# Where the operands of a matmul begin in SBUF: stationary tiles at multiples of 256 bytes, four ring slots at four different offsets

## The chip, the cores and the metric

The kernel runs on one core of one Trainium2 chip. The time is the device time of one launch in microseconds (us); of several runs the median is given. Beside it stands the span of one profiled execution, from the first to the last instruction of the program on that core.

## The reference

One layer of a decoder trunk on a sequence of 256 tokens of width 2048, all in float32:

```python
h = h + 0.5 * rms_norm(swiglu(rms_norm(h, w1), w_gate, w_up, w_down), w2)   # ffn1, D_FF = 5504
h = h + rms_norm(hybrid_token_mixer(rms_norm(h, w3), ...), w4)              # w_in is 2048 x 11280
h = h + 0.5 * rms_norm(swiglu(rms_norm(h, w5), w_gate, w_up, w_down), w6)   # ffn2
```

`swiglu(x)` is `(silu(x @ w_gate) * (x @ w_up)) @ w_down`. The mixer projects with `w_in`, runs two causal gated linear attentions (one with 4 heads, one with 8), normalises and gates their outputs, projects each with a 1024 x 2048 matrix (`w_branch_gla`, `w_branch_hgrn`), mixes the two with sigmoid gates and projects with `w_out` (2048 x 2048). Nearly all arithmetic is in the products of 256 tokens with these weight matrices.

## The kernel before

**Tiles.** The 256 tokens are two halves of 128 (`t` = 0, 1). A product `x @ w` is made in blocks of 512 output columns (`CB`): for each half, the block is one PSUM tile of 128 x 512, summed over the rows of `w` in steps of 128 (`kt`). TensorE holds a 128 x 128 piece of the transposed activations as its stationary operand and streams 512 columns of weights past it as the moving operand.

**Three matmuls per step.** Every float32 operand is split into a high part in the fp32r format and the rest, also fp32r (`split_into`, L118: ScalarE makes the high part at L119, VectorE the rest at L120). A product is then three matmuls (`mm3`, L122): high activations with high weights (L124), low activations with high weights (L125), high activations with low weights (L126). Each matmul is preceded on TensorE by the load of its stationary operand, which the profile shows as LDWEIGHTS on PEld. The three matmuls of one step have the stationary pieces `xhi`, `xlo`, `xhi` of the same `kt`, so the load that runs beside a matmul is always one for the next matmul's piece.

**The ring.** Weights come in chunks of 256 rows by 512 columns (`wchunk`, L105): one DMA of 512 KB into `raw`, then the split into `whi` and `wlo`. These three tags live in the pool `ring` with `bufs=4` (L80): each tag has four slots, side by side in each partition, and the chunks use them in turn. A chunk feeds 12 matmuls: 2 rows of 128, 2 halves of tokens, 3 matmuls each (`gemm_block`, L128, from L149; in `out_proj`, L248, a chunk is 128 rows by 1024 columns, again 12 matmuls). Some chunks of a product that has to wait for the second half's activations are kept longer, in tiles named `held`, outside the ring.

**The stationary operands.** `xhi` and `xlo` (`new_xT`, L192) hold the transposed input of a stage: 16 pieces of 128 columns, 512 bytes each in a partition. In the down projections of the FFNs the stationary operands are `hkhi` and `hklo` (L392 in `ffn`), in the two branch projections of the mixer they are the tiles `oT` (in `attention`, from the pool `b2`).

**Where these lie.** A pool places its tiles in the order in which they are allocated, and a tag's slot is as large as the tag's largest tile. The largest `whi` is that of the mixer's product of 16 + 512 columns: 2 x 528 x 4 = 4224 bytes = 16 x 256 + 128. A partition of SBUF is laid out so (bytes; the last column is the rest after division by 256):

| tiles | first bytes | mod 256 |
|---|---|---|
| `xhi`, `xlo` | 34048, 42240, 50432, 58624 | 0 |
| `whi`, four slots | 83712, 87936, 92160, 96384 | 0, 128, 0, 128 |
| `wlo`, four slots | 100608, 104832, 109056, 113280 | 0, 128, 0, 128 |
| `hkhi`, `hklo` | 167040, ... 181376 | 128 |
| `oT` and the mixer's `held` | 164000, ... | 160 |
| the FFNs' `held` | 183424, ... | 128 |

All pieces of a stationary tile and both halves of a ring tile are a multiple of 256 bytes apart, but for the one product of 528 columns (parts of 264 columns, 1056 bytes). The **offset** of a matmul is in what follows the first byte of its moving operand less that of the stationary operand which is loaded beside it, mod 256. With `xhi` at 0 the four slots have the offsets 0, 128, 0, 128; with `hkhi` at 128 they have 128, 0, 128, 0; with `oT` at 160 they have 96, 224, 96, 224.

**What sets the order.** The order of instructions on each engine is that in which the code issues them, with waits on tiles added by the framework; small jobs (norms, transposes, the attention) are generators that `Side` runs a step at a time between the chunks.

Of the kernel before, what the change touches and what calls it, by code (L numbers as in the profile page):

```python
# [7 lines left out]
F32 = mybir.dt.float32  # L8
F32R = mybir.dt.float32r
# [6 lines left out]
P = 128  # L16
D = 2048
NT = 2
KT = D // P
# [3 lines left out]
CB = 512  # L23
GATE_NORMALIZER = 16.0
LEVELS = (1, 2, 4, 8, 16, 32, 64)
TAIL = 4
STEPS = ((5, 3, 3, 3), (7, 3, 2, 2))
O_GQ, O_GK, O_GV, O_GO, O_CODE = 0, 512, 1024, 2048, 3072
O_HQ, O_HF, O_HI, O_HO, O_ZG, O_ZH = 3088, 4112, 5136, 6160, 7184, 9232
# [41 lines left out]
def kernel(ctx: ExitStack, tc: tile.TileContext, a: dict, out: bass.AP):  # L71
    nc = tc.nc
    side = Side()

    const = ctx.enter_context(tc.tile_pool(name="const", bufs=1))
    hpool = ctx.enter_context(tc.tile_pool(name="hpool", bufs=1))
    tpool = ctx.enter_context(tc.tile_pool(name="tpool", bufs=1))
    ring = ctx.enter_context(tc.tile_pool(name="ring", bufs=4))
    rows = ctx.enter_context(tc.tile_pool(name="rows", bufs=8))
    small = ctx.enter_context(tc.tile_pool(name="small", bufs=4))  # L80
    work = ctx.enter_context(tc.tile_pool(name="work", bufs=2))
# [4 lines left out]
    def nm(s):  # L86
        uid[0] += 1
        return f"{s}_{uid[0]}"

    def ps_tile(s="ps"):  # L90
        return psum.tile([P, CB], F32, tag="ps", name=nm(s))

    h = [[hpool.tile([P, CB], F32, name=f"h{t}_{n}") for n in range(4)] for t in range(NT)]
    ident = const.tile([P, P], F32, name="ident")
    nc.scalar.dma_start(ident, a["c_ident"])
    nhalf = const.tile([P, 4], F32, name="nhalf")
    nc.vector.memset(nhalf, -0.5)


    def ring_alloc(w):  # L100
        hi = ring.tile([P, 2, w], F32R, tag="whi", name=nm("whi"))
        lo = ring.tile([P, 2, w], F32R, tag="wlo", name=nm("wlo"))
        return [(hi, lo)]

    def wchunk(src: bass.AP, w: int, alloc=ring_alloc):  # L105

        raw = ring.tile([P, 2, w], F32, tag="raw", name=nm("raw"))
        nc.sync.dma_start(raw, src)
        parts = alloc(w)
        if len(parts) == 1:  # L110
            split_into(*parts[0], raw)
            hi, lo = parts[0]
            return [(hi[:, i, :], lo[:, i, :]) for i in range(2)]
        for i, (hi, lo) in enumerate(parts):
            split_into(hi, lo, raw[:, i, :])
        return parts
# [11 lines left out]
    def gemm_block(w_dram, c0, w, lhs, nkt=KT, held=None):  # L128
# [19 lines left out]
        if held is None:  # L148
            for k0 in range(0, nkt, 2):  # L149
                parts = chunk(k0, ring_alloc)  # L150
                for t in range(NT):
                    mm(t, k0, parts)
                side.pump()
        else:
            kept = []
            for i, k0 in enumerate(range(0, nkt, 2)):
                kept.append((k0, chunk(k0, ring_alloc if i < 4 else held)))
                mm(0, *kept[-1])
                side.pump()
            for k in kept:  # L160
                mm(1, *k)
                side.pump()
            side.flush()
# [89 lines left out]
    def out_proj(w_dram, nkt, lhs, post, scale, pre, held, after):  # L253
# [15 lines left out]
        def load(kt, hf, alloc=ring_alloc):  # L269
            return wchunk(w_dram[kt * P:(kt + 1) * P, hf * 1024:(hf + 1) * 1024]  # L270
                          .rearrange("p (n c) -> p n c", n=2), CB, alloc)

        def mm(t, n, kt, parts):
            if acc[t][n] is None:
                acc[t][n] = ps_tile(f"acc{t}{n}")
            mm3(acc[t][n], lhs(t, kt), parts[n % 2], kt == 0, kt == nkt - 1)

        order = [(kt, hf) for hf in range(2) for kt in range(2)]
        order += [(kt, hf) for kt in range(2, nkt - TAIL) for hf in range(2)]
        for i, (kt, hf) in enumerate(order):  # L280
# [6 lines left out]
            if i > 3 and early:  # L287
                o, x0, x1 = early.pop(0)
                nc.vector.tensor_tensor(o, x0, x1, op=ALU.mult)
        tail = [[(kt, load(kt, hf, held if hf else ring_alloc)) for kt in range(nkt - TAIL, nkt)]  # L290
                for hf in range(2)]
# [6 lines left out]
        def finish(t, ss):  # L298
# [23 lines left out]
            def ahead(n):  # L322
                tmp = scaled_acc(t, n, r1, wpre[n])
                nc.vector.tensor_tensor(u[t][n], u[t][n], tmp, op=ALU.add)
                if t == 0:
                    settle(n)
                    square(h[t][n], ss2, n)

            ahead(0)
            ahead(1)  # L330
            for n, steps in enumerate(STEPS[t]):
                for _ in range(steps):
# [10 lines left out]
        for t in range(NT):  # L343
            ss = small.tile([P, 4], F32, tag="ss", name=nm("ss"))
            for n in range(4):
                for i, (kt, parts) in enumerate(tail[n // 2]):
                    mm(t, n, kt, parts)
                    if i == TAIL // 2 - 1:
                        side.pump()
# [58 lines left out]
    def mixer(x, rs):  # L408
        xl = lhs_of(x)
        w_in = a["w_in"]  # L410
        with ExitStack() as mctx:
            mp = mctx.enter_context(tc.tile_pool(name="mp", bufs=1, reuse_waits="tile"))
            b2 = mctx.enter_context(tc.tile_pool(name="b2", bufs=1, reuse_waits="tile"))
            oT, state = {}, {}

# [343 lines left out]
            return out_proj(a["w_out"], KT, lhs_of(mT), "mix_post_norm", 1.0, "ffn2_pre_norm", held, after)  # L759


    warm = const.tile([P, 1], F32, name="warm")
    nc.scalar.activation(warm, nhalf[:, 0:1], AF.Silu)
    wrow = const.tile([KT, P], F32, name="wrow")
    nc.scalar.dma_start(wrow, a["ffn1_pre_norm"][0].rearrange("(k p) -> k p", p=P))
    wcol = const.tile([P, KT], F32, name="wcol")
    tp = ps_tile()
    nc.tensor.transpose(tp[:, :KT], wrow, ident[:KT, :KT])
    nc.vector.tensor_copy(wcol, tp[:, :KT])
# [1 line left out]
    for t in range(NT):  # L771
        side.spawn(first_norm(t, x, rs, wcol))
    x, rs = ffn("ffn1", x, rs, "ffn1_post_norm", "mix_pre_norm")
    x, rs = mixer(x, rs)
    ffn("ffn2", x, rs, "ffn2_post_norm", None)
    side.flush()
# [46 lines left out]
```

## Time and profile before

| | |
|---|---|
| median of 3 runs | 2230.61 us (2230.21 to 2231.8) |
| the profiled execution's own time | 2231.95 us |
| its span | 2230.2 us |
| mean granted TensorE clock | 0.999 |
| VectorE, ScalarE, GpSimd busy | 53%, 45%, 3% of the span |
| DMA | 410.24 MB, mean 184 GB/s |

The profile groups instructions by line, engine and tiles (`mm<-whi,xhi` is a matmul into the PSUM tile `mm` with `whi` moving and `xhi` stationary). In the timeline each row begins with the start in us and the duration in us. The ends of matmuls are modelled and overlap the next one's start, so the cost of a matmul is read from start to start: the time from one row's start to that of the 12th row after it, divided by 12, is the pitch of a chunk's matmuls.

### The profile page before, as it was taken

Reading aid. Unit: us, or ns where it says so; the run is one execution under the profiler, and the core shown is the slowest. Engines: PE = TensorE matmul, PEld = TensorE weight load, DVE = VectorE, ACT = ScalarE, POOL = GpSimd, SP = SyncE. Lnnn points to the kernel's source line nnn. Section 1 sums busy time; section 2 is a strip of 40 time slices with the busy share of each in tenths; the row PEclk is TensorE's granted clock in tenths of the full one; section 3 lists DMA queues with packets and bytes.
Section 4 is the critical chain, followed back from the end, with each engine's and each line's share of the span. In section 5 each row is a group of like instructions: output and inputs, shape, how many; then the busy total and the mean of one; then the engine's idle time right before and its main releaser. Section 6 shows DMA issues by size and latency. Waiting matters only on the chain.

```text
span 2230.2 us, 26313 instructions
## 1 busy us (share of the span) xinstructions
PE 2203.3 (99%) x10197; PEld 1815.4 (81%) x10197; DVE 1184.1 (53%) x1278; ACT 994.3 (45%) x1202; POOL 69.2 (3%) x106
## 2 busy tenths in 40 slices
PE   8999999999999999999999999999999999999998
PEld 6888888897888788888888888878888888898886
DVE  5544444446445744657575656465444444444455
ACT  5444444444444564444434444354444444444443
POOL 0000000000000400000000000021000000000001
PEclk9999999999999999999999999999999999999999
DMA  6655555566555556554545765555555565566663
GB/s 228 189 184 186 188 188 185 187 204 205 191 189 197 160 172 189 170 150 143 155 153 175 232 204 184 184 166 182 189 186 187 184 189 189 170 217 190 191 192 135
DMA packets 189344, 410.24 MB, mean 184 GB/s; under 512 B 13681, under 2 KB 22289, under 8 KB 189218
## 3 DMA queue, kind: packets, MB, share of 16 engines
q1 hardware_dynamic: 183712, 400.21, 57.0%
q10 hardware_dynamic: 5506, 8.34, 1.2%
q8 instruction: 80, 1.31, 0.2%
q14 instruction: 46, 0.38, 0.0%
HBM read 406.41 MB, written 2.10 MB: 183 GB/s over the span
## 4 chain that ended last, share of the span: by engine, by line
PE 64%; DVE 1%; DMA 1%; POOL 1%; ACT 0%; issue 0%; ACTq 0%; POOLq 0%; DVEq 0%
PE mm L124 16%; PE mm L126 16%; PE mm L125 16%; PE acc L126 5%; PE acc L124 5%; PE acc L125 5%; PE ps L187 1%; PE ps L531 1%; DMA raw<-in_w_out_dram 0%; PE ps L581 0%; PE ps L538 0%; PE ps L515 0%; DVE tmp L295 0%; DVE wlo L120 0%; DMA raw<-in_w_in_dram 0%; POOL h L303 0%
## 5 line engine op out<-in xcount | busy, mean ns | idle before, releaser
L120 DVE TENSOR_TENSOR wlo<-raw,whi 128x1024 fp32r<-128x1024 f32 (+2 forms) x740 | 899.5, 1217 | 916.0 <-ACT whi L119 880.2
L119 ACT ACTIVATE whi<-raw 128x1024 fp32r<-128x1024 f32 (+2 forms) x740 | 777.3, 1051 | 1134.2 <-PE mm L125 814.9
L124 PE MATMUL mm<-whi,xhi 128*128 128x512 f32 (+2 forms) x2096 | 817.1, 390 | 3.5 <-ACT whi L119 3.3
L126 PE MATMUL mm<-wlo,xhi 128*128 128x512 f32 (+2 forms) x2096 | 810.1, 387 | 5.5 <-DVE wlo L120 5.5
L125 PE MATMUL mm<-whi,xlo 128*128 128x512 f32 (+2 forms) x2096 | 809.0, 386 | 0.2
L126 PEld LDWEIGHTS mm<-wlo,xhi 128*128 128x128 f32 x2096 | 393.7, 188 | 87.3 <-DVE wlo L120 7.2
L124 PEld LDWEIGHTS mm<-whi,xhi 128*128 128x128 f32 x2096 | 394.1, 188 | 83.1 <-ACT whi L119 3.7
L125 PEld LDWEIGHTS mm<-whi,xlo 128*128 128x128 f32 x2096 | 394.4, 188 | 79.9 <-DVE xlo L120 1.6
L124 PE MATMUL acc<-whi,hkhi 128*128 128x512 f32 x656 | 257.5, 392 | 0.8 <-ACT hT L376 0.8
L126 PE MATMUL acc<-wlo,hkhi 128*128 128x512 f32 x656 | 257.5, 393 | 0.0
L125 PE MATMUL acc<-whi,hklo 128*128 128x512 f32 x656 | 257.3, 392 | 0.0
L124 PEld LDWEIGHTS acc<-whi,hkhi 128*128 128x128 f32 x656 | 123.2, 188 | 28.8 <-ACT hT L376 1.2
L126 PEld LDWEIGHTS acc<-wlo,hkhi 128*128 128x128 f32 x656 | 123.1, 188 | 28.1 <-DVE wlo L120 0.2
L125 PEld LDWEIGHTS acc<-whi,hklo 128*128 128x128 f32 x656 | 123.1, 188 | 27.9
L217 POOL TENSOR_TENSOR v<-ss 128x1 f32<-128x1 f32 x12 | 6.2, 518 | 1693.2 <-ACT sq L228 1692.4
L124 PE MATMUL mm<-whi,oT 128*128 128x512 f32 x128 | 51.3, 401 | 0.0
L126 PE MATMUL mm<-wlo,oT 128*128 128x512 f32 x128 | 50.7, 396 | 0.0
L125 PE MATMUL mm<-whi,oT 128*128 128x512 f32 x128 | 50.6, 395 | 0.0
L124 PE MATMUL acc<-whi,xhi 128*128 128x512 f32 x112 | 44.1, 394 | 0.0
L125 PE MATMUL acc<-whi,xlo 128*128 128x512 f32 x112 | 44.0, 393 | 0.0
L126 PE MATMUL acc<-wlo,xhi 128*128 128x512 f32 x112 | 44.0, 393 | 0.0
L385 ACT ACTIVATE silu<-mm,r 128x512 f32<-128x512 f32 (+1 forms) x44 | 29.5, 670 | 18.3 <-PE mm L126 15.3
(196 smaller groups left out, 1130.5 us busy)
## 6 DMA issues: line engine op xcount, KB each, us to landing
raw<-in_ffn_w_down_dram SPq DMA_DIRECT2D x172, 512.0 KB, 4.6
raw<-in_w_in_dram SPq DMA_DIRECT2D x168, 512.0 KB, 3.6
raw<-in_ffn_w_gate_dram SPq DMA_DIRECT2D x160, 512.0 KB, 3.4
raw<-in_ffn_w_up_dram SPq DMA_DIRECT2D x160, 512.0 KB, 3.4
raw<-in_w_out_dram SPq DMA_DIRECT2D x32, 512.0 KB, 4.5
raw<-in_w_branch_gla_dram SPq DMA_DIRECT2D x16, 512.0 KB, 3.6
raw<-in_w_branch_hgrn_dram SPq DMA_DIRECT2D x16, 512.0 KB, 3.9
raw<-in_ffn_w_gate_dram SPq DMA_DIRECT2D x16, 384.0 KB, 3.1
```

The source lines that it names most:

```text
L119: nc.scalar.activation(hi, src, AF.Copy)
L120: nc.vector.tensor_tensor(lo, src, hi.bitcast(F32), op=ALU.subtract)
L124: nc.tensor.matmul(ps, lhsT=xhi, rhs=whi, start=start, stop=False)
L125: nc.tensor.matmul(ps, lhsT=xlo, rhs=whi, start=False, stop=False)
L126: nc.tensor.matmul(ps, lhsT=xhi, rhs=wlo, start=False, stop=stop)
L187: nc.tensor.transpose(dst_ps[:, i * P:(i + 1) * P], src[:, i * P:(i + 1) * P], ident)
L217: nc.gpsimd.tensor_tensor(v[:, 0:1], ss[:, 0:1], ss[:, 1:2], op=ALU.add)
L385: after = nc.scalar.activation(st[:, :w], g[t][:, :w], AF.Silu, scale=rs[t])
L531: nc.tensor.matmul(ps[:, i * 64:(i + 1) * 64], lhsT=kT[:, sl], rhs=halves(qT[:, sl])[1], start=True, stop=True)
```

## The change

Nothing is computed otherwise, and every engine has the same instructions in the same order; one wait at the program's start is added (below). What changes is where tiles begin.

```diff
+LINE = 256
+RW = (2 * CB * 4 + 192) // 4
...
     h = [[hpool.tile([P, CB], F32, name=f"h{t}_{n}") for n in range(4)] for t in range(NT)]
+    nhalf = const.tile([P, 4], F32, name="nhalf")
+    nc.vector.memset(nhalf, -0.5)
+    warm = const.tile([P, 1], F32, name="warm")
+    wcol = const.tile([P, KT], F32, name="wcol")
     ident = const.tile([P, P], F32, name="ident")
     nc.scalar.dma_start(ident, a["c_ident"])
-    nhalf = const.tile([P, 4], F32, name="nhalf")
-    nc.vector.memset(nhalf, -0.5)
+    small.tile([P, 32], F32, tag="fill", name="fill", bufs=1)
...
     def ring_alloc(w):
-        hi = ring.tile([P, 2, w], F32R, tag="whi", name=nm("whi"))
-        lo = ring.tile([P, 2, w], F32R, tag="wlo", name=nm("wlo"))
+        hi, lo = [ring.tile([P, RW], F32R, tag=s, name=nm(s))[:, :2 * w]
+                  .rearrange("p (i c) -> p i c", i=2) for s in ("whi", "wlo")]
         return [(hi, lo)]
...
             mp = mctx.enter_context(tc.tile_pool(name="mp", bufs=1, reuse_waits="tile"))
+            mp.tile([P, 56], F32, name="mfill")
...
-    warm = const.tile([P, 1], F32, name="warm")
     nc.scalar.activation(warm, nhalf[:, 0:1], AF.Silu)
-    wrow = const.tile([KT, P], F32, name="wrow")
+    wrow = work.tile([P, CB], F32, tag="tmp", name="wrow", bufs=3)[:KT, :P]
     nc.scalar.dma_start(wrow, a["ffn1_pre_norm"][0].rearrange("(k p) -> k p", p=P))
-    wcol = const.tile([P, KT], F32, name="wcol")
```

A slot of `whi` or `wlo` is now 2 x 512 x 4 + 192 = 4288 bytes long, 16 x 256 + 192, whatever the width of the chunk. The tiles `fill` and `mfill` are never used; they move what is allocated behind them. The small constants and `wrow` are allocated elsewhere for the same reason. `wrow` (16 x 128, the first norm's weights, read once at the start) shares a buffer with the first stage's work tiles, and the third of these, `u` of the first norm, waits for it as well. The layout is then:

| tiles | first bytes | mod 256 |
|---|---|---|
| `xhi`, `xlo` | 33536, 41728, 49920, 58112 | 0 |
| `whi`, four slots | 83200, 87488, 91776, 96064 | 0, 192, 128, 64 |
| `wlo`, four slots | 100352, 104640, 108928, 113216 | 0, 192, 128, 64 |
| `hkhi`, `hklo` | 167168, ... 181504 | 0 |
| `oT` and both kinds of `held` | 164352, ..., 183552, ... | 0 |

So a chunk's matmuls have the offset 0, 64, 128 or 192, a quarter of the chunks each, in all stages, and the matmuls with `held` tiles have the offset 0.

## Prediction

> **What bounds the kernel now.** I read the head of the page first, then the matmuls of one line by tiles, then the starts of matmuls in the timeline.
>
> ```profile
> span 2230.2 us, 26313 instructions
> ## 1 busy us (share of the span) xinstructions
> PE 2203.3 (99%) x10197; PEld 1815.4 (81%) x10197; DVE 1184.1 (53%) x1278; ACT 994.3 (45%) x1202; POOL 69.2 (3%) x106
> ```
>
> TensorE is busy for 99% of the span and every other engine for about half of it. So the time is the number of matmuls times their pitch, and anything that leaves the pitch alone leaves the time alone. How many there are, by line L124 (first of the three matmuls of a step; L125 and L126 have as many):
>
> ```profile
> L124 PE MATMUL mm<-whi,xhi x2096: 281/392/792, 9.6 to 1980.6; 128*128 128x512 f32 x173, 128*128 128x384 f32 x12, 128*128 128x264 f32 x6
> L124 PE MATMUL acc<-whi,hkhi x656: 388/392/498, 501.1 to 2213.3; 128*128 128x512 f32 x164
> L124 PE MATMUL mm<-whi,oT x128: 388/395/483, 1137.4 to 1397.1; 128*128 128x512 f32 x128
> L124 PE MATMUL acc<-whi,xhi x112: 388/392/486, 1397.9 to 1482.4; 128*128 128x512 f32 x112
> L124 PE MATMUL mm<-held,xhi x48: 390/395/499, 22.1 to 1518.9; 128*128 128x512 f32 x48
> L124 PE MATMUL acc<-held,hkhi x32: 389/391/478, 723.9 to 2218.8; 128*128 128x512 f32 x32
> L124 PE MATMUL acc<-held,xhi x16: 390/397/497, 1470.7 to 1488.5; 128*128 128x512 f32 x16
> ```
>
> Of the 2096, 128 have 384 columns (the last block of the FFNs: 2 layers x 2 products x 16 x 2 halves) and 64 have 264 (16 x 2 x 2 parts); 1904 have 512. From the ring then come 3 x (1904 + 656 + 128 + 112) = 8400 matmuls of 512 columns, 384 of them with `oT`, 8016 with the other stationary tiles; 3 x (48 + 32 + 16) = 288 have `held` tiles.
>
> Now the pitch. Two chunks of an up projection (`xhi` at 0 mod 256): the first has offset 0, the second 128.
>
> ```profile
> 298.19 0.39 PE L124 MATMUL mm<-whi,xhi 128*128 128x512 f32 x1
> 298.42 0.40 PE L125 MATMUL mm<-whi,xlo 128*128 128x512 f32 x1
> 298.66 0.39 PE L126 MATMUL mm<-wlo,xhi 128*128 128x512 f32 x1
> 298.89 0.39 PE L124 MATMUL mm<-whi,xhi 128*128 128x512 f32 x1
> ...
> 300.93 0.40 PE L124 MATMUL mm<-whi,xhi 128*128 128x512 f32 x1
> ...
> 303.72 0.39 PE L124 MATMUL mm<-whi,xhi 128*128 128x512 f32 x1
> ```
>
> 12 matmuls take 2.74 us at offset 0 (228.3 ns each) and 2.79 us at offset 128 (232.5 ns). Within the first chunk, three matmuls take 0.70 us (233 ns each), and the other nine 2.04 us (226.7 ns): at offset 0 the pitch needs three matmuls to settle, and then stays low. That this belongs to the offset and not to a slot is seen in the down projection, where the stationary tiles lie at 128, so that the slots at 128 have offset 0. The first chunk here is in such a slot (96384), the second in one at 0 mod 256 (92160, offset 128):
>
> ```profile
> 560.91 0.39 PE L124 MATMUL acc<-whi,hkhi 128*128 128x512 f32 x1
> ...
> 563.64 0.40 PE L124 MATMUL acc<-whi,hkhi 128*128 128x512 f32 x1
> ...
> 566.43 0.39 PE L124 MATMUL acc<-whi,hkhi 128*128 128x512 f32 x1
> ```
>
> 2.73 and 2.79 us again: the slots have changed sides with the stationary operand. I take 227.9 ns for offset 0 (5.47 us by 24 matmuls, both stages) and 232.5 ns for offset 128. Two branch projections of the mixer (`oT` at 160) show offsets 96, 224 and 96 again:
>
> ```profile
> 1217.42 0.39 PE L124 MATMUL mm<-whi,oT 128*128 128x512 f32 x1
> ...
> 1220.22 0.39 PE L124 MATMUL mm<-whi,oT 128*128 128x512 f32 x1
> ...
> 1223.01 0.40 PE L124 MATMUL mm<-whi,oT 128*128 128x512 f32 x1
> ...
> 1225.83 0.40 PE L124 MATMUL mm<-whi,oT 128*128 128x512 f32 x1
> ```
>
> 2.80, 2.79 and 2.82 us: 233.3 ns, 232.5 ns and 235.0 ns. And the second half's pass over the mixer's `held` tiles (at 160, with `xhi` at 0: offset 160), first and last start of 24 matmuls:
>
> ```profile
> 766.24 0.40 PE L124 MATMUL mm<-held,xhi 128*128 128x512 f32 x1
> ...
> 771.62 0.39 PE L126 MATMUL mm<-held,xhi 128*128 128x512 f32 x1
> ```
>
> 23 pitches in 5.38 us are 233.9 ns. So four offsets that are not 0 (96, 128, 160, 224) cost 232.5 to 235.0 ns, and offset 0 alone costs 227.9 ns.
>
> [...]
>
> **The change part by part.** No instruction is added, removed or moved, no DMA is larger, and no tile's slots become fewer, so all of the cost is in pitches. Everything is summed as a difference, so it holds for the profiled execution (2231.95 us, 1.3 us above the median) as for the median, to which I add it.
>
> *The ring, 8016 matmuls with `xhi`, `xlo`, `hkhi`, `hklo`.* Before, half of them (4008) have offset 0 and half offset 128. After, a quarter each (2004) has 0, 64, 128 and 192. So 2004 go from offset 0 to an offset of 64 or 192, 2004 from offset 128 to one of these, and the rest stay. What 64 and 192 cost, no matmul of 512 columns shows. The lower bound is the pitch of offset 0, 227.9 ns (nothing in the trace is below it over a chunk), the upper the dearest chunk above, 235.0 ns. I take 233.0 ns, the mean of 232.5 (offset 128), 233.3 (the first at 96), 232.5 (224) and 233.9 (160), since these surround 64 and 192 on both sides, while only the exact offset 0 is cheap. 2004 x (233.0 - 227.9) = 10.2 us, and 2004 x (233.0 - 232.5) = 1.0 us: +11.2 us.
>
> The two offsets do occur once, in the mixer's product of 264-column parts. Its three matmuls at 64 begin with the first row, those at 192 with the third; the second and the fourth row end them:
>
> ```profile
> 774.44 0.29 PE L124 MATMUL mm<-whi,xhi 128*128 128x264 f32 x1
> ...
> 774.80 0.28 PE L124 MATMUL mm<-whi,xhi 128*128 128x264 f32 x1
> ...
> 776.77 0.28 PE L124 MATMUL mm<-whi,xhi 128*128 128x264 f32 x1
> ...
> 777.14 0.28 PE L124 MATMUL mm<-whi,xhi 128*128 128x264 f32 x1
> ```
>
> 0.36 and 0.37 us for three, 120 and 123 ns. The starts have steps of 10 ns and the offset changes every three matmuls, which is as long as offset 0 needs to settle: these rows don't decide between the bounds. I read them only as no sign of something far outside.
>
> *The 384 matmuls with `oT`.* Before, (233.3 + 232.5) / 2 = 232.9 ns; after, a quarter each at 0, 64, 128 and 192: (227.9 + 233.0 + 232.5 + 233.0) / 4 = 231.6 ns. -0.5 us.
>
> *The 288 matmuls with `held` tiles.* All come to offset 0. 96 (FFN gate projections, 128 against 0) go from 232.5 to 227.9 ns, -0.4 us; 96 (both mixer products, 160) from 233.9 to 227.9 ns, -0.6 us; 96 in the down projections are at 0 already. -1.0 us.
>
> *The 384 matmuls of 384 columns.* A quarter of them (96) leaves offset 0; at the same 5 ns each +0.5 us, and nothing if shorter matmuls feel it less.
>
> *The rest* has one answer: transposes and attention matmuls are a small part of the PE rows, and their order and waits stay. The extra wait of the third `u` on `wrow`'s DMA and readers lies at the program's start, behind the transpose of `wrow`, which stands first in TensorE's order and which `u` needs anyway through `wcol`: 0.
>
> Sum: 11.2 - 0.5 - 1.0 + 0.5 = +10.2 us, and 2230.6 + 10.2 = 2240.8 us, 0.46% slower.
>
> **The rivals.**
>
> *One of the two new offsets settles like offset 0.* The settling at offset 0 suggests that the load and the stream fall into step there; another offset could have such a step of its own. Then 4008 / 2 = 2004 matmuls cost 5.1 ns less than I took, -10.2 us, and the time is 2230.6 us: no change. For it: the pitch of offset 0 is a state that is reached, not a price paid per byte. Against it: 96, 128, 160 and 224 have none.
>
> *Both do: faster.* If what counts is whether the two streams begin at a multiple of 64 bytes and half a period is the one exception, then 64 and 192 cost 227.9 ns, and 4008 x 5.1 = 20.4 us fall away: 2220.4 us. The place is the ring's slots at 64 and 192 in every stage. It decides from the pitch at which the ring's two terms cancel the small gains: 2004 x (p - 227.9) + 2004 x (p - 232.5) = 1.0, p = 230.4 ns; below that the change gains. For it: 96, 160 and 224 are all odd multiples of 32, so 128 is the only offset at a multiple of 64 that the trace has shown dear. Against it: that one is dear, and no more cheaply so than the odd ones (232.5 against 232.5 to 235.0).
>
> *Both are dearer than any sampled so far.* At 235.0 ns the sum grows by 4008 x 2.0 = 8.0 us, to 2248.8 us. For it: 96 had chunks of 233.3 and 235.0 ns, so a mean of an offset may hide more than one state. Against it: three other offsets stay under 234 ns.
>
> [...]
>
> **How the numbers follow.** Forecast (new offsets at 232 to 235 ns) 0.67, one of them cheap 0.12, both cheap 0.13, dearer than 235 ns 0.05, no dependence 0.03. A measurement of this kernel can tell about 0.2%, 4.5 us, from no change. Slower by more than that: 0.67 + 0.05 = 0.72. Within it: 0.12 + 0.03 = 0.15. Faster: 0.13. The range has to hold 8 in 10: from 2229 (one cheap, no dependence) to 2248 us (just under both at 235.0 ns) it holds 0.67 + 0.12 + 0.03 = 0.82, and leaves out both cheap and the dearest. The forecast alone has the range 2237 to 2248 us.
>
> **What would show it.** In the profile after, the starts of chunks in an FFN's up projection, four in a row in the order 0, 64, 128, 192: I expect 2.74, 2.80, 2.79 and 2.80 us for 12 matmuls each. In the down projection the same four, now that its stationary tiles are at 0. In the branch projections one chunk in four at 2.74 us, where none was. TensorE stays at 99% and the counts of instructions stay. The prediction is wrong if the chunks at 64 and 192 take under 2.76 us (230.4 ns each), or if the chunks at offset 0 lose their low pitch because another offset now comes before them, which would add at most 2004 x 5 = 10 us to the sum. It is wrong in its ground if a chunk's time no longer goes with its offset.

## The result, and the profile after

| | before | changed |
|---|---|---|
| median of 13 runs each | 2230.93 us | 2236.31 us |
| lowest to highest | 2229.1 to 2233.29 | 2234.93 to 2238.38 |
| profiled execution | 2231.95 us | 2237.24 us |
| its span | 2230.2 us | 2235.5 us |

The changed kernel takes 1.0024 times as long, with a 95% interval of 1.0015 to 1.0033: slower by 5.4 us, where 10.2 us were forecast. The head of its page:

```profile
span 2235.5 us, 26314 instructions
## 1 busy us (share of the span) xinstructions
PE 2208.8 (99%) x10197; PEld 1817.6 (81%) x10197; DVE 1184.2 (53%) x1278; ACT 994.2 (44%) x1202; POOL 69.1 (3%) x106
```

TensorE has the same 10197 matmuls and is busy for 5.5 us longer; VectorE, ScalarE and GpSimd changed by 0.1 us each. The one instruction more is a semaphore wait of VectorE, the added wait at the start. So the loss is in the pitch. The timeline of TensorE in the changed kernel, in an up projection: starts of chunks at the offsets 0, 64, 128 and 192, of the next at 0, and of a chunk at 0 eight chunks (96 matmuls) after the first row:

```profile
298.84 0.39 PE L131 MATMUL mm<-whi,xhi 128*128 128x512 f32 x1
...
301.58 0.40 PE L131 MATMUL mm<-whi,xhi 128*128 128x512 f32 x1
...
304.34 0.40 PE L131 MATMUL mm<-whi,xhi 128*128 128x512 f32 x1
...
307.14 0.39 PE L131 MATMUL mm<-whi,xhi 128*128 128x512 f32 x1
...
309.93 0.39 PE L131 MATMUL mm<-whi,xhi 128*128 128x512 f32 x1
...
321.02 0.39 PE L131 MATMUL mm<-whi,xhi 128*128 128x512 f32 x1
```

2.74, 2.76, 2.80 and 2.79 us for 12 matmuls: 228.3, 230.0, 233.3 and 232.5 ns. Three are as forecast to the 0.01 us of the rows (2.74, 2.79 and 2.80 us for 0, 128 and 192). The offset 64 was to take 2.80 us and takes 2.76. In the kernel before, the row eight chunks after the one at 298.19 (shown in the prediction) is

```profile
320.30 0.39 PE L124 MATMUL mm<-whi,xhi 128*128 128x512 f32 x1
```

so 96 matmuls took 22.11 us before (230.3 ns each) and take 22.18 us now (231.0 ns): 0.7 ns more per matmul, and 8016 of them make +5.9 us, where 0.01 us in a row is worth 0.8 us. The down projection of the changed kernel, a chunk at offset 64:

```profile
562.10 0.40 PE L131 MATMUL acc<-whi,hkhi 128*128 128x512 f32 x1
...
564.87 0.40 PE L131 MATMUL acc<-whi,hkhi 128*128 128x512 f32 x1
```

2.77 us, the same as in the up projection within the 0.01 us of the rows. In a branch projection of the mixer, a chunk at offset 0, which no chunk had there before:

```profile
1226.56 0.39 PE L131 MATMUL mm<-whi,oT 128*128 128x512 f32 x1
...
1229.30 0.40 PE L131 MATMUL mm<-whi,oT 128*128 128x512 f32 x1
```

2.74 us, where the chunks in this place took 2.79 to 2.82 us.

### The profile page after: what moved, and what is told of

The parts are those of the page before. It is cut to its first block, busy times and chain, and to the rows that moved or that the text cites. A ratio compares the mean times of both kernels' runs of the same rounds, so it can differ in the third digit from the quotient of the medians.

```text
span 2235.5 us, 26314 instructions
## 1 busy us (share of the span) xinstructions
PE 2208.8 (99%) x10197; PEld 1817.6 (81%) x10197; DVE 1184.2 (53%) x1278; ACT 994.2 (44%) x1202; POOL 69.1 (3%) x106
## 4 chain that ended last, share of the span: by engine, by line
PE 64%; DVE 1%; POOL 1%; DMA 0%; issue 0%; ACT 0%; ACTq 0%; POOLq 0%; DVEq 0%
PE mm L131 16%; PE mm L133 15%; PE mm L132 15%; PE acc L131 5%; PE acc L133 5%; PE acc L132 5%; PE ps L539 1%; PE ps L194 1%; PE ps L589 0%; PE ps L546 0%; DMA raw<-in_w_out_dram 0%; DVE tmp L302 0%; POOL h L310 0%; PE ps L523 0%; POOL v L225 0%
```

## The experiments

The theory: a matmul's pitch goes with the offset between the operand that streams and the one that is loaded beside it; each offset has a pitch to which the matmuls settle, and a change of offset from chunk to chunk costs a few matmuls of settling. The rivals: only the changes of offset cost, and any constant offset would be cheap; the place of one operand alone counts; or something else with a period of a few chunks makes the difference. All experiments start from the changed kernel, and their ratios are to the kernel before, run on the same chip. They ran in three rounds, each on a chip of its own, on which the kernel before took 2232.13, 2232.19 and 2232.05 us, so that times of different rounds may be set side by side.

**One offset for the whole ring.** A slot of 4352 bytes (17 x 256) puts all four slots at the same offset:

```diff
-RW = (2 * CB * 4 + 192) // 4
+RW = (2 * CB * 4 + 256) // 4
```

That is the whole edit for offset 0. For 64 and 128 an unused tile of that many bytes is allocated ahead of `whi`, and `fill` is shortened so that what lies behind stays at its place mod 256; here for 64:

```diff
-    small.tile([P, 32], F32, tag="fill", name="fill", bufs=1)
+    small.tile([P, 16], F32, tag="fill", name="fill", bufs=1)
...
+        if not shift:
+            shift.append(ring.tile([P, 16], F32, tag="shift", name="shift", bufs=1))
```

For 192 the unused tile has 48 columns and each slot is a tile of its own, the last one shorter, as the layout would not fit otherwise.

> All four slots of the ring at the offset 0 (slots of 4352 bytes). Theory (the pitch goes with the offset between moving and stationary operand, and a change of offset from chunk to chunk costs a few matmuls of settling): the 8400 ring matmuls fall from the changed kernel's mean of about 231.1 ns (228.5, 230.3, 232.9, 232.9 at 0, 64, 128, 192) to the settled 226.7 ns, with interruptions 227.0: 8400 x -4.1 = -35 us, 2201 us. First rival (only the change of offset between chunks costs): 2201 as well. Second rival (the split of weights on ScalarE and VectorE or the DMAs make the difference between chunks): 2236, as the changed kernel.

Measured: 2202.91 us, ratio 0.9869 [0.9854, 0.9884].

> All four slots at the offset 64. Theory: the changed kernel's chunks at 64 settle into 231.6, 225.8, 229.2 ns, mean 228.9; with interruptions 229.2: 8400 x (229.2 - 231.1) = -16 us, 2220 us. First rival (only changes of offset cost): 2201. Second rival: 2236.

Measured: 2221.04 us, ratio 0.9949 [0.9933, 0.9966].

> All four slots at the offset 128. Theory: two settled patterns were seen at 128, 237.5 and 229.2 in turn (mean 233.3, kernel before) and one of seven matmuls (mean 232.3, changed kernel): 8400 x 1.2 to 2.2 = +10 to +18 us, 2246 to 2255 us. First rival: 2201. Second rival: 2236.

Measured: 2247.25 us, ratio 1.0069 [1.0054, 1.0084].

> All four slots at the offset 192 (each slot is a tile of its own, so that the layout fits). Theory: settled at 233.3 ns: 8400 x 2.2 = +18 us, 2255 us. First rival: 2201. Second rival: 2236.

Measured: 2253.86 us, ratio 1.0099 [1.0084, 1.0114].

The theory's four numbers were 2201, 2220, 2246 to 2255 and 2255 us. Both rivals fall: a constant offset of 128 or 192 is dearer than any mixture run, and ScalarE, VectorE and the DMAs have the same work in all four kernels (VectorE is busy for 1183.0 to 1184.5 us, ScalarE for 993.3 to 994.7 us). In the timeline the settled pitch is read from two starts 180 matmuls apart, inside one long run of a gate and an up projection. With all at 0:

```profile
198.62 0.39 PE L132 MATMUL mm<-whi,xlo 128*128 128x512 f32 x1
...
239.42 0.39 PE L132 MATMUL mm<-whi,xlo 128*128 128x512 f32 x1
```

With all at 64:

```profile
200.47 0.39 PE L136 MATMUL mm<-whi,xlo 128*128 128x512 f32 x1
...
241.66 0.39 PE L136 MATMUL mm<-whi,xlo 128*128 128x512 f32 x1
```

With all at 128:

```profile
203.54 0.39 PE L135 MATMUL mm<-whi,xlo 128*128 128x512 f32 x1
...
245.38 0.39 PE L135 MATMUL mm<-whi,xlo 128*128 128x512 f32 x1
```

With all at 192:

```profile
203.03 0.40 PE L139 MATMUL mm<-whi,xlo 128*128 128x512 f32 x1
...
245.03 0.40 PE L139 MATMUL mm<-whi,xlo 128*128 128x512 f32 x1
```

40.80, 41.19, 41.84 and 42.00 us: 226.7, 228.8, 232.4 and 233.3 ns. Times 8400 matmuls, the last three are 18, 49 and 56 us above the first; measured are 18, 44 and 51 us. Most of the excess comes from taking the settled pitch for all matmuls: over all pairs of neighbouring ring matmuls in the traces (pauses of 300 ns and more left out) the means are 227.0, 229.1, 232.4 and 233.3 ns, so the two low pitches are interrupted now and then and the two high ones lose nothing by it; with these the three are 18, 45 and 53 us above the first. TensorE stays the bound with all at 0:

```profile
PE 2175.3 (99%) x10197; PEld 1816.0 (82%) x10197; DVE 1183.0 (54%) x1278; ACT 994.7 (45%) x1202; POOL 69.2 (3%) x106
```

This kernel, at 2202.91 us, is the fastest of the study, 1.3% under the kernel before.

**The stationary tiles alone.** The ring's stride goes back to that of before, the stationary tiles stay at multiples of 256 bytes:

```diff
-RW = (2 * CB * 4 + 192) // 4
+RW = (2 * CB * 4 + 128) // 4
```

> The stationary tiles at multiples of 256 bytes as in the change, the ring's slots at 0 and 128 as before (slots of 4224 bytes). Theory: only the 384 matmuls with oT (232.9 to 230.2 ns: -1.0 us) and 192 of those with held tiles (-1.0 us) get cheaper: 2 us under the kernel before. A rival that puts the change's loss down to the moved stationary tiles or the small moves at the start: 5 us over it.

Measured: 2231.27 us beside 2232.19 us of the kernel before, ratio 0.9994 [0.9985, 1.0003]. That is -0.9 us, with an interval from -3.3 to +0.7 us: it holds the theory's -2 us and no change, and excludes that the stationary tiles or the small moves at the start cost the change its 5 us. The size of this gain itself is not shown.

**The slots in the other order.** Each slot is a tile of its own, allocated in the order of its use:

```diff
+        k = len(turn) % 4
+        turn.append(k)
+        hi, lo = [ring.tile([P, n[k] // 4], F32R, tag=f"{s}{k}", name=nm(s), bufs=1)[:, :2 * w]
+                  .rearrange("p (i c) -> p i c", i=2)
+                  for s, n in (("whi", HI_BYTES), ("wlo", LO_BYTES))]
```

> The change with the slots used in the order 0, 192, 128, 64 instead of 0, 64, 128, 192 (each slot a tile of its own). Theory: the settled pitches stay, only the first three or so of each 12 matmuls differ: the changed kernel's time within 4 us. Rival (the order of the offsets decides): further off than that.

Measured: 2236.93 us, ratio 1.0019 [1.0010, 1.0028], not to be told from the change's 1.0024 (2236.31 us). Its timeline, chunks at the offsets 0, 192, 128 and 64:

```profile
299.22 0.39 PE L136 MATMUL mm<-whi,xhi 128*128 128x512 f32 x1
...
301.97 0.39 PE L136 MATMUL mm<-whi,xhi 128*128 128x512 f32 x1
...
304.77 0.39 PE L136 MATMUL mm<-whi,xhi 128*128 128x512 f32 x1
...
307.56 0.39 PE L136 MATMUL mm<-whi,xhi 128*128 128x512 f32 x1
...
310.31 0.39 PE L136 MATMUL mm<-whi,xhi 128*128 128x512 f32 x1
```

2.75, 2.80, 2.79 and 2.75 us. The chunk at 64 costs 0.01 us less when it comes after 128 than when it comes after 0, the one at 0 costs 0.01 us more; that is the resolution of the rows. The offsets themselves decide, and their order hardly: 2236.93 us beside 2236.31.

**Both operands at 64, and the stationary one alone at 192.** The first is the kernel with all at 0 and an unused tile of 64 bytes ahead of `xhi`, so that ring, `xhi`, `xlo`, `hkhi`, `hklo`, `oT` and `held` all lie at 64:

```diff
+    tpool.tile([P, 16], F32, tag="tfill", name="tfill")
```

> Ring and all stationary tiles at 64 mod 256, offset 0 everywhere. Theory (only the offset between the two operands counts): as with all at 0, 2203 us. Rival (what counts is that an operand begins at a multiple of 256 bytes): not under 2221, the time with the ring alone at 64.

Measured: 2203.67 us, ratio 0.9870 [0.9857, 0.9884], as with all at 0 (2202.91). In the second the ring lies at 0 and all stationary tiles at 192, which is an offset of 64:

```diff
+    tpool.tile([P, 48], F32, tag="tfill", name="tfill")
-    small.tile([P, 32], F32, tag="fill", name="fill", bufs=1)
+    small.tile([P, 16], F32, tag="fill", name="fill", bufs=1)
...
+            shift.append(ring.tile([P, 16], F32, tag="shift", name="shift", bufs=1))
```

> The ring at 0, all stationary tiles at 192 mod 256: offset 64 reached from the other side. Theory: as with the ring at 64, 2221 us. Rival (the stationary operand's own place counts, as the change's words have it): another time than that, at 192 rather that of the ring at 192, 2254.

Measured: 2220.32 us, ratio 0.9947 [0.9933, 0.9960], as with the ring at 64 and the stationary tiles at 0 (2221.04). That an operand begins at a multiple of 256 bytes is worth nothing by itself here; the difference of the two is what counts.

**How narrow the cheap offset is.** The kernel with all at 0, with the ring's tiles begun 16 or 32 bytes into their slots (for 240, slots of their own behind a larger unused tile):

```diff
-        hi, lo = [ring.tile([P, RW], F32R, tag=s, name=nm(s))[:, :2 * w]
+        hi, lo = [ring.tile([P, RW], F32R, tag=s, name=nm(s))[:, 4:4 + 2 * w]
```

> The ring 16 bytes past a multiple of 256, offset 16 in all its matmuls: how narrow is the cheap offset? If the low pitch is a state that is fallen into and has some width, 226.7 ns still and 2203 us; if it needs the exact offset, a pitch as at the others, 229 to 233.4 ns: 2221 to 2254 us.

Measured: 2241.04 us, ratio 1.0041 [1.0026, 1.0056].

> The ring at the offset 32. If the pitch rises evenly from 0 (226.7 ns) to 64 (228.9 ns): 227.8 ns, 2212 us. If only 0 is settled: 229 ns or more, 2221 us or more. If the odd multiples of 32 are all dear, as 96, 160 and 224 were: 233 ns, 2253 us.

Measured: 2254.16 us, ratio 1.0100 [1.0083, 1.0116]. The pitch doesn't rise evenly; the time is that of the last expectation, all odd multiples of 32 dear. Over 180 matmuls:

```profile
203.04 0.39 PE L132 MATMUL mm<-whi,xlo 128*128 128x512 f32 x1
...
245.04 0.39 PE L132 MATMUL mm<-whi,xlo 128*128 128x512 f32 x1
```

42.00 us, 233.3 ns, as with all at 192.

> The ring 16 bytes short of a multiple of 256, offset 240 (each slot a tile of its own). If the cheap state has some width on both sides: 2203 us. If the offsets below 0 join those at 192 and 224 (233 ns): 2253 us.

Measured: 2272.98 us, ratio 1.0183 [1.0168, 1.0199], dearer than either expectation. 16 bytes to either side cost 38 and 70 us. At 240 there are two settled pitches, one after the other in the same profile, each again over 180 matmuls:

```profile
158.15 0.40 PE L138 MATMUL mm<-whi,xlo 128*128 128x512 f32 x1
...
200.75 0.40 PE L138 MATMUL mm<-whi,xlo 128*128 128x512 f32 x1
...
204.43 0.40 PE L138 MATMUL mm<-whi,xlo 128*128 128x512 f32 x1
...
246.43 0.40 PE L138 MATMUL mm<-whi,xlo 128*128 128x512 f32 x1
```

42.60 us and 42.00 us: 236.7 and 233.3 ns.

## Why the prediction came out as it did

*The bound* was read rightly: the time followed the pitch of the matmuls in every kernel of the study; with all at 0, TensorE is still busy for 99% of the span and no other engine for more than 54%.

*That the offset between the two operands sets the pitch* was right, and is now shown rather than read out of two stages: moving both by 64 bytes changes nothing (2203.67 us beside 2202.91), moving either one by the same difference costs the same (2221.04 us with the ring moved, 2220.32 us with the stationary tiles moved). In this stream of fp32r matmuls, each with a load beside it (10197 of each on the page), addresses alone move the kernel from 2202.91 to 2272.98 us. By what mechanism they do so, the runs don't show.

*The sizes at 0, 128 and 192* held: 228.3, 233.3 and 232.5 ns a chunk in the changed kernel, against 227.9, 232.5 and 233.0 ns taken; each is within 0.8 ns, the resolution of a chunk's rows.

*The step that was mis-sized* is the price of the offset 64. The prediction put it at 233.0 ns, "since these surround 64 and 192 on both sides, while only the exact offset 0 is cheap". Measured in the changed kernel are 2.76 and 2.77 us for a chunk, 230.4 ns a matmul. 2004 x (230.4 - 233.0) = -5.2 us, which accounts for the 4.8 us between the 10.2 us forecast and the 5.4 us measured. So the time lies in the prediction's range, but just under the 2237 to 2248 us that it gave for its forecast alone, and the chunks at 64 stand at the 230.4 ns that it named as the sign of being wrong. That the change still lost is due to 192, which was priced by the same argument; as that argument failed at 64, its success at 192 was in part luck. The first rival (one of the two new offsets settles as well) was thus partly true: 64 has a settled pattern of its own, but at 228.8 ns and not at 226.7, and the change of offset in each chunk adds to it. The error lay in reading prices between sampled offsets as if they varied evenly. They don't: 0, 16, 32 and 64 settle at 226.7, 231.7, 233.3 and 228.8 ns.

*The small terms*, -0.5 us for `oT` and -1.0 us for the `held` tiles, are within what the run with the stationary tiles alone allows, but are not shown; nor are the +0.5 us of the narrower matmuls.

*The rival with both offsets cheap* fell with 192, which is the same at 232.5 ns in the change and 233.3 ns alone. *The rival of dearer offsets* (more than one state at an offset) is real at 240, which this change doesn't use, with 233.3 and 236.7 ns, and in a small way at 128 (over the last ten matmuls of the chunk at 128 in the kernel before 233.3 ns, with all at 128 232.4 ns); no state dearer than 235 ns came up at 64 and 192 in the chunks shown.

## What to carry to other kernels

When TensorE is the bound (99% busy here) and every matmul has a load of a stationary operand beside it, read the pitch from start to start, chunk by chunk: a period in it that goes with the buffers' slots, as the 2.74 and 2.79 us in turn of the kernel before, is a sign that addresses matter. Here the moving and the stationary operand had to have the same place mod 256, the cheapest of the seven offsets that the whole ring was given (0, 16, 32, 64, 128, 192, 240), and that was worth 1.3% (2202.91 us, ratio 0.9869). It took two things: slots padded by 128 bytes, so that all have one place, and the stationary tiles of every stage moved to that same place. The second without the first was worth 0.15% at most by its interval; the first without the second was not run. Spreading the slots over four offsets was the wrong remedy here, where one offset is cheap and its neighbours are not: it cost 5.4 us, and one offset for all, 0, gained 29.2 us. And an offset that wasn't measured couldn't be priced by those around it: 64, taken at 233.0 ns, took 230.4.

## What the runs showed of the hardware that was not expected

The cheap offset is narrow: 16 bytes off cost 4.5 to 8.3 ns per matmul (38 and 70 us by 8400). The settled pitches are of a common measure: 40.80 and 42.00 us for 180 matmuls are 34 and 35 times 6.67 ns each, and 42.60 us are 35.5 times, a whole number for two matmuls. With all at 16 it is a quarter:

```profile
202.48 0.39 PE L132 MATMUL mm<-whi,xlo 128*128 128x512 f32 x1
...
244.18 0.39 PE L132 MATMUL mm<-whi,xlo 128*128 128x512 f32 x1
```

41.70 us are 34.75 times 6.67 ns, a whole number for four. The 41.84 us with all at 128 are 34.9 times 6.67 ns; the trace of the changed kernel has a pattern of seven matmuls at this offset (in the chunk at 304.34 us 241, 232, 231, 232, 228, 230 and 233 ns), which take 1627 ns, 244 times 6.67 ns. So a whole number of steps of 6.67 ns is taken by one, two, three, four or seven matmuls. The single starts are not bound to such steps: in its chunk at 64 (301.58 us) the distances settle at 226, 230 and 231 ns in turn, and only the three together, 687 ns, are 103 steps. What the 6.67 ns are, the runs don't tell.
